# RWKV recurrence: ScalarE's instructions kept in program order, with loads, splits, statistics and one buffer rearranged

## The chip, the core and the metric

The kernel runs on one core of a Trainium2 chip. The metric is the device time of one execution in microseconds (us). The engines are named as in the profile: PE is TensorE (PEld its weight loads), DVE is VectorE, ACT is ScalarE, POOL is GpSimd, and SP is SyncE, whose queue issues the DMAs. A line number such as L1520 is a line of the kernel before the change.

## The reference

The reference is one inference step of a two-layer decoder trunk on 1,104 tokens: 8 sample sequences of 8 tokens, 16 meta tokens and a prompt of 1,024 tokens. Layer 0 is a gated DeltaNet, layer 1 is RWKV-7. The change touches the second half of layer 1 only: the recurrence over the tokens, the normalisation of its output, the output projection, and the final norm. What it computes, per head of 64 channels:

```python
def step(S, inp):
    r_t, k_t, v_t, d_t, kk_t, b_t = inp
    S = (S * d_t[:, :, None, :]
         + jnp.einsum('bhvk,bhk->bhv', S, -kk_t)[..., None] * b_t[:, :, None, :]
         + v_t[..., None] * k_t[:, :, None, :])
    return S, jnp.einsum('bhvk,bhk->bhv', S, r_t)

S, y = lax.scan(step, S0.astype(jnp.float32), (tm(r_h), tm(k_h), tm(v_h), tm(d_h), tm(kk), tm(b_h)))
...
y = (y - mean) * lax.rsqrt(var + GN_EPS) * lnx_w.reshape(H, N) + lnx_b.reshape(H, N)
y = y + jnp.sum(r_h * k_h * r_k, -1, keepdims=True) * v_h
y = y.reshape(B, T, D) * jax.nn.silu(z)
return y @ w_o, S, xn[:, -1]
```

The residual is added to the result, and a final RMSNorm gives the outputs.

## The kernel before

**Stages.** Layer 0 and the projections of layer 1 fill the first 1,890 us or so. Then comes `wave` (L1832), which is where the change lies. It works on 24 units: 3 segments of the tokens (`SEGS`, 384, 384 and 336 columns) times 8 pairs of heads. A unit has 6 chunks of 64 tokens. Step `tau` of the wave works on up to three units at once: unit n enters at step 2n and takes one chunk in each of six steps, so there are 52 steps (0 to 51), after some that only prepare.

**One step.** `step_solve` (L1457) multiplies the keys with the states S into a PSUM tile X, which ACT copies (L1478). `parts[0]` then computes half the score matrices of a coming unit on PE (`scores`, tile `G`; DVE masks them, L1386 and L1388). `step_inner` multiplies X by a triangular inverse `rTT` and ACT writes the result, UV (L1490). `step_old` scales the old states on ACT (`pre`, L1499). `step_state` (L1501) multiplies UV into new states and outputs; DVE writes the states (L1520), ACT copies the outputs y (L1528) into a ring of 8 steps. `parts[1]` and `parts[2]` hold the rest of a coming unit's preparation: the bonus term (L1371), transposed values and keys (ACT copies, L1410 and L1397).

**A unit's front and finish.** `rwkv_front` (L1330) is a generator. Up to its first `yield` (L1358) it issues the four loads of a unit (`fld2c`, `fldrv`, `AR`, `BK`), two exponentials on ACT (`fDp`, `fiD`, L1247 and L1248) and two products on DVE (L1353, L1356). It runs at the end of each even step (`front`, L1938). Its second part, one step later, makes `pr` on DVE and splits it in two on ACT and POOL (L1362, L1364). `rwkv_finish` (L1530) begins at the end of a unit's last step: twelve statistics instructions on DVE (L1540, L1541), a power of -0.5 on POOL (L103) and three DVE instructions of a Newton step (L104 to L106), then `gnm` (L1546). In the next steps ACT normalises six pieces of y (L1549), PE transposes them (`fyT`), DVE applies gain, bonus and gate (L1558, L1559), and `split` makes the two halves that the projection reads.

**Samples.** For the first 8 units, `rwkv_sample_read` loads the sample sequences' states in 8 DMAs (`sn`, L1579), and `rwkv_sample_write` (L1604) spreads UV over the sequences (`ue`, one half on POOL and one on DVE, L1609), multiplies (`drsw`, L1614), updates the states on DVE, transposes them, copies them on ACT (L1623) and stores them in 8 DMAs (L1627). The copy uses a tile of the tag `ue`, which has two buffers in all.

**Work that fills the steps.** `jobs` and `more` (L1861, L1865) are generators with a start and an end in units of `tau`; `fill(now)` advances each in proportion. They are the last gate projection (`gate_tiles`, PSUM tile `zz`, result `zst`), the output projection (`project_out`, tiles `zo` and `do`) and the final norm (`finish`). Their weights come from `stream` (L209): each block of weights is loaded into `wraw` (two buffers), ACT rounds it to `whi`, and POOL computes the rest `wlo` (three buffers each).

**What sets the order.** PE's instructions keep the order in which the program names them: the wave stands in `with tc.manual_schedule(engines={mybir.EngineType.PE})` (L1826). For all other engines, and for SP's DMAs, the compiler's scheduler picks at each point of a simulated timeline the ready instruction that was named first, and waits are inserted between engines. On the chip each engine runs its own list in order. `tc.high_priority()` lets a few instructions go ahead.

Of the kernel before, what the change touches and what calls it, by code (L numbers as in the profile page):

```python
# [7 lines left out]
F32R = mybir.dt.float32r  # L8
# [27 lines left out]
class Builder:  # L36
# [8 lines left out]
    def t(self, pool, shape, tag, bufs=1, dt=F32):  # L45
        self.uid += 1
        return pool.tile(shape, dt, name=f"{tag}_{self.uid}", tag=tag, bufs=bufs)
# [41 lines left out]
        e = nc.gpsimd if eng_lo == "pool" else nc.vector  # L89
        e.tensor_tensor(lo, x, hi.bitcast(F32), op=ALU.subtract)  # L90

    def rsqrt(self, y, x, pool, tag, bufs=2):

        v = self.nc.vector
        p0, sh = x.start_partition(), list(x.shape)
        n = 1
        for d in sh[1:]:
            n *= d
        t = self.t(pool, [p0 + sh[0], n], tag + "_t", bufs)[p0:p0 + sh[0]]
        t = t.rearrange("p (a b) -> p a b", b=sh[2]) if len(sh) == 3 else t  # L100
        half = self.cv(-0.5, p0, sh[0])
        half = half.unsqueeze(2) if len(sh) == 3 else half
        self.nc.gpsimd.tensor_tensor(y, x, half.broadcast_to(sh), op=ALU.pow)  # L103
        v.tensor_tensor(t, y, y, op=ALU.mult)  # L104
        v.scalar_tensor_tensor(t, t, -0.5, x, op0=ALU.mult, op1=ALU.mult)
        v.scalar_tensor_tensor(y, t, 1.5, y, op0=ALU.add, op1=ALU.mult)  # L106
# [82 lines left out]
    def load_w(self, src, kt=8, into=None):  # L189

        nc = self.nc
        n = src.shape[1]
        v = src.rearrange("(k p) m -> p k m", p=128)
        his, los = [], []
        for h in range(0, kt, 4):
            w = self.t(self.wp, [128, 4, 128], "wraw", 2)
            m = min(4, kt - h)
            nc.sync.dma_start(w[:, 0:m, 0:n], v[:, h:h + m, :])
            if into:
                hi, lo = into[0][h // 4], into[1][h // 4]  # L200
            else:
                hi = self.t(self.wp, [128, 4, 128], "whi", 3, F32R)
                lo = self.t(self.wp, [128, 4, 128], "wlo", 3, F32R)
            self.split(w[:, 0:m, 0:n], hi[:, 0:m, 0:n], lo[:, 0:m, 0:n], eng_lo="dve" if into else "pool")
            his.append(hi)
            los.append(lo)
        return his, los

    def stream(self, srcs):  # L209

        w = []
        for n in range(len(srcs)):
            for q in range(len(w), min(n + 3, len(srcs))):
                w.append(self.load_w(srcs[q], srcs[q].shape[0] // 128))
            yield w[n][0][0], w[n][1][0]

    def dense(self, w, m, xh, xl, seg, kt=8, tag="d", bufs=2, label=""):

# [1111 lines left out]
    def rwkv_front(self, p, s):  # L1330

        nc, t, ap, fp, col = self.nc, self.t, self.ap, self.fp, self.pcol
        P = Ctx()
        P.p, P.s, P.n = p, s, 8 * s + p
        NB = self.NB
# [4 lines left out]
        def system():  # L1340
            nc.sync.dma_start(P.TT.rearrange("p c k -> p (c k)"), self.ttd[(P.n + 1) // 5][:, 384 * (P.n - max(5 * ((P.n + 1) // 5) - 1, 0)):][:, 0:384])
        ld = self.rwkv_load(P.n, fp, "f", ("2c", "rv"))
        Dp, iD = self.rwkv_decays(ld, fp, "f")
        DC = P.DC = t(fp, [128, 14], "DC", NB + 2)
        nc.gpsimd.tensor_copy(DC[:, 0:6].unsqueeze(2), Dp[:, 1:385].rearrange("p (c k) -> p c k", k=64)[:, :, 63:64])
        if s == 0:
            nc.gpsimd.tensor_copy(DC[:, 6:14].unsqueeze(2), Dp[:, 1:65].rearrange("p (c k) -> p c k", k=8)[:, :, 7:8])
        AR = P.AR = t(fp, [128, 2, 6, 64], "AR", NB + 1)
        BK = t(fp, [128, 6, 2, 64], "BK", 2)
        nc.sync.dma_start(AR[:, 0].rearrange("p c k -> p (c k)"), self.abd[P.n][:, 0:384])  # L1350
        nc.sync.dma_start(BK[:, :, 1, :], self.abd[P.n][:, 384:768].rearrange("p (c k) -> p c k", k=64))
# [149 lines left out]
    def step_state(self, W):  # L1501
# [25 lines left out]
        if lo < hi:  # L1527
            nc.scalar.copy(y[:, lo:hi].rearrange("p c k -> p (c k)"), W.pY[:, 64 * lo:64 * hi])  # L1528

    def rwkv_finish(self, p, s, P):  # L1530

        nc, t, ap, col = self.nc, self.t, self.ap, self.pcol
        c0, n = SEGS[s]
        y = lambda q: self.ring_y(2 * P.n + q)[:, 2 - q // 2]
        zg = t(ap, [128, 384], "lz", 2)
        nc.sync.dma_start(zg, self.zd[p][:, c0:c0 + 384])
        st = t(ap, [128, 6, 6], "bnst", 2)
        mv = t(ap, [128, 6, 2], "mv", 2)
        for q in range(6):
            nc.vector.bn_stats(st[:, q, :], y(q))  # L1540
            nc.vector.bn_aggr(mv[:, q, :], st[:, q, :])  # L1541
        va, rs = t(ap, [128, 6], "va", 2), t(ap, [128, 6], "grs", 2)
        nc.vector.tensor_scalar(va, mv[:, :, 1], GN_EPS, None, op0=ALU.add)
        self.rsqrt(rs, va, ap, "gn")
        nm = t(ap, [128, 6], "gnm", 2)
        nc.vector.scalar_tensor_tensor(nm, mv[:, :, 0], -1.0, rs, op0=ALU.mult, op1=ALU.mult)  # L1546
        yield
        for q in range(6):
            self.act(y(q), y(q), AF.Identity, scale=rs[:, q:q + 1], bias=nm[:, q:q + 1])  # L1549
            if q in (3, 5):  # L1550
                yield
        yp = self.ps("f", 2, "yT")
        for q in range(6):
            for h in (0, 64):
                g = 64 - h
                self.mm(yp[h:h + 64, 64 * q:64 * q + 64], y(q)[g:g + 64], self.ident[g:g + 64, g:g + 64])
        t1 = t(self.fp, [128, 384], "k2", 1)
        nc.vector.scalar_tensor_tensor(t1[:, 0:n], yp[:, 0:n], self.lnw[:, p:p + 1], P.bv[:, 0:n], op0=ALU.mult, op1=ALU.add)  # L1558
# [45 lines left out]
    def rwkv_sample_write(self, p, P, BT, DC):  # L1604
        nc, t, ap = self.nc, self.t, self.ap
        UV = self.ring_uv(2 * P.n)[:, 2]
        ue = [t(self.fin, [128, 8, 64], "ue", 2) for h in (0, 1)]
# [11 lines left out]
        op = self.ps("d", 2, "sbT")  # L1619
        for g in range(4):  # L1620
            self.transpose(op[:, 128 * g:128 * g + 128], P.Sb[:, 2 * g:2 * g + 2, :].rearrange("p b k -> p (b k)"))
        so = t(self.fin, [128, 4, 2, 64], "ue", 2)
        nc.scalar.copy(so.rearrange("p g h k -> p (g h k)"), op)  # L1623
        st = self.o["s_rwkv"][0].rearrange("(g u) h v k -> u v g h k", u=2)
        for u in (0, 1):
# [37 lines left out]
    def finish(self, s, x2):  # L1663
        nc, t, i, o, fp = self.nc, self.t, self.i, self.o, self.fin
        for q in range(3):
            tt = 3 * s + q
            nr = 80 if tt == 8 else 128
            tag = [("d", 2), ("f", 2), ("r", 3)][q] if s == 2 else ("d", 2)
# [7 lines left out]
            r, rs = t(self.fin2, [128, 1], "fr", 2), t(self.fin2, [128, 1], "frs", 2)  # L1676
            nc.vector.tensor_tensor(r[0:nr], r2[0:nr, 0:1], r2[0:nr, 1:2], op=ALU.add)
            nc.vector.tensor_scalar(r[0:nr], r[0:nr], 1.0 / D, RMS_EPS, op0=ALU.mult, op1=ALU.add)
            self.rsqrt(rs[0:nr], r[0:nr], self.fin2, "fn")
            yp, ys = o["y_prompt"][0], o["y_sample"].rearrange("b r d -> (b r) d")  # L1680
            for h in (0, 1):
                hs = slice(512 * h, 512 * h + 512)
# [109 lines left out]
    def layer1(self, ctx, right, stay, xa, xb, x):  # L1792

        nc, tc = self.nc, self.tc
# [28 lines left out]
        self.ys = t(ap, [128, self.RING, 3, 64], "y")  # L1823
        self.TTz = [t(ap, [128, 6, 64], f"rTT{q}") for q in range(3)]
        nc.vector.memset(self.UVs, 0.0)
        with tc.manual_schedule(engines={mybir.EngineType.PE}):  # L1826
            self.wave(zin, stay, last, pool)
        last.close()
        ctx.close()
# [2 lines left out]
    def wave(self, zin, stay, last, pool):  # L1832
# [22 lines left out]
        def norms(s):  # L1855
            x = self.sums_in(s)
            yield
            yield
            yield from self.finish(s, x)
# [2 lines left out]
                (lambda: out(2, Z), 16, 30, 38), (lambda: out(3, DD), 16, 38, 46), (lambda: out(4, Z), 16, 46, 51),  # L1862
                (lambda: out(5, DD, x2), 16, 52.1, 54), (lambda: out(6, DD, x2), 8, 54.1, 55), (lambda: self.finish(2, x2), 4, 55, 56)]

        more = [(lambda: norms(0), 5, 31, 36), (lambda: norms(1), 5, 47, 51), (lambda: x2.extend(self.sums_in(2)) or iter(()), 1, 51.6, 52)]  # L1865
        runs = {}

        def fill(now):
# [15 lines left out]
                    del runs[id(jl)]  # L1884

        late = []
        def front(tau):

            if tau % 2 and (tau + 3) // 2 < 24:
                s, p = divmod((tau + 3) // 2, 8)  # L1890
                begun.append(self.rwkv_front(p, s))
                P[8 * s + p] = next(begun[-1])

        begun = []
        front(-3)
        for tau in range(-3, 55):
            m = (tau + 2) // 2
            parts = P[m].parts[3 * (tau % 2):3 * (tau % 2) + 3] if 0 <= m < 24 else [[], [], []]
# [10 lines left out]
            with self.tc.issue_after(ins) if W else ExitStack():  # L1909
# [31 lines left out]

# [28 lines left out]
```

## Time and profile before

| | us |
|---|---|
| median of 3 runs (2340.41 to 2344.61) | 2343.65 |
| the profiled execution | 2352.16 |
| its span, first to last instruction | 2350.4 |
| PE busy, of the span | 2161.4 |
| ACT busy | 1272.2 |
| DVE busy | 1603.1 |
| first and last ACT copy of X in the wave (steps 1 and 51) begin at | 1898.9 and 2304.7 |

Times inside the execution are counted from the span's start. "Busy" is the time in which an engine had an instruction in work, and the busy times of engines overlap. A row of the timeline gives the start, the duration, the engine, the line, the operation, the tile written and the tiles read, shapes, a count, and in brackets how long the engine was idle before it and what ended that. A row of the waits gives who waited for whom, the total in us, the number of times and the longest. A row of the windows gives, for one stretch of time, each engine's busy time and count of instructions, then the granted PE clock (1.00 is full), the share of DMA time used and GB/s.

### The profile page before, as it was taken

To read this page: it belongs to the slowest core of one execution; us is meant where nothing else is said; L and a number is where in the kernel's file an instruction comes from. 1 tells how busy PE (TensorE), PEld (TensorE's weight loads), DVE (VectorE), ACT (ScalarE), POOL (GpSimd) and SP (SyncE) were. 2 spreads that over 40 slices of the span, in tenths; PEclk is the share of its full clock that TensorE was granted. 3 is DMA by queue.
4 is the path that set the end of the run, shared out by engine and by line. 5 is a ranking of instruction groups with operands and counts; after the bars stand their busy time and mean duration, and the time that the engine had idled before them with its cause. 6 is when DMAs were issued, how large, how long until landed. Compare 5 with 4: busy or idle time off the path is not lost. (4 is left out here: it accounts for less than half of the span.)

```text
span 2350.4 us, 55277 instructions
## 1 busy us (share of the span) xinstructions
PE 2161.4 (92%) x20452; PEld 1966.9 (84%) x20452; DVE 1603.1 (68%) x4224; ACT 1272.2 (54%) x3642; POOL 926.3 (39%) x1267
## 2 busy tenths in 40 slices
PE   6989999999999999999999999988889988999986
PEld 5888989989888889888998989888778966788875
DVE  6868768685858677684336765878969355677754
ACT  5445555465554655566433554746545345577763
POOL 3435334343434334444231442644434333344443
PEclk9999999999999999999999999999989989999998
DMA  3324233423333333327244146654552644577754
GB/s 113 99 75 112 80 90 79 110 62 101 87 89 108 88 92 76 106 76 199 68 130 114 55 123 216 201 162 146 154 150 79 192 114 131 161 224 224 209 163 135
DMA packets 433128, 293.37 MB, mean 125 GB/s; under 512 B 148329, under 2 KB 415706, under 8 KB 432858
## 3 DMA queue, kind: packets, MB, share of 16 engines
q1 hardware_dynamic: 432858, 289.84, 43.0%
q8 instruction: 161, 2.64, 0.5%
q14 instruction: 109, 0.89, 0.1%
HBM read 198.02 MB, written 91.71 MB: 123 GB/s over the span
## 5 line engine op out<-in xcount | busy, mean ns | idle before, releaser
L90 POOL TENSOR_TENSOR wlo<-wraw,whi 128x512 fp32r<-128x512 f32 (+2 forms) x252 | 332.0, 1320 | 367.1 <-ACT whi L86 346.6
L76 PE MATMUL d<-xc,whi 128*128 128x384 f32 (+2 forms) x910 | 263.7, 346 | 7.0 <-DVE key L1168 2.2
L86 ACT CAST whi<-wraw 128x512 fp32r<-128x512 f32 (+2 forms) x252 | 151.7, 604 | 123.8 <-PE dq L76 50.5
L415 DVE SCALAR_TENSOR_TENSOR cvy<-raw,cw,cvy 128x408 f32<-128x408 f32 (+2 forms) x288 | 179.6, 637 | 17.1 <-ACT cvy L62 15.3
L76 PEld LDWEIGHTS d<-xc,whi 128*128 128x128 f32 (+1 forms) x910 | 170.9, 194 | 14.3 <-issue 4.1
L451 DVE TENSOR_TENSOR invtmp<-invA,invT 72x31 f32<-72x31 f32 (+31 forms) x403 | 167.0, 414 | 11.4 <-DMA invA<-ltd 4.6
L453 DVE TENSOR_TENSOR invT<-invT,invtmp 72x31 f32<-72x31 f32 (+31 forms) x403 | 170.1, 422 | 6.7
L76 PE MATMUL dz<-xc,whi 128*128 128x384 f32 (+1 forms) x480 | 150.1, 344 | 0.0
L76 PE MATMUL dv<-xc,whi 128*128 128x384 f32 (+1 forms) x480 | 146.7, 334 | 0.0
L76 PE MATMUL d<-xc,wlo 128*128 128x384 f32 (+2 forms) x428 | 145.5, 346 | 0.5 <-POOL wlo L90 0.5
L76 PE MATMUL d<-xa,whi 128*128 128x384 f32 (+3 forms) x450 | 142.1, 349 | 3.2 <-DVE xa L90 1.8
L815 POOL TENSOR_SCALAR Sb<-Sb,eglb 128x128 f32<-128x128 f32 x128 | 80.5, 648 | 89.8 <-DMA Sb<-in_state_gdn 39.5
L76 PE MATMUL dz<-xa,whi 128*128 128x384 f32 (+1 forms) x288 | 101.3, 352 | 0.0
L76 PE MATMUL dv<-xa,whi 128*128 128x384 f32 (+1 forms) x288 | 99.9, 347 | 0.1
L76 PEld LDWEIGHTS d<-xa,whi 128*128 128x128 f32 (+1 forms) x450 | 85.5, 194 | 7.9 <-issue 2.4
L76 PEld LDWEIGHTS dz<-xc,whi 128*128 128x128 f32 x480 | 90.2, 193 | 0.8
L76 PEld LDWEIGHTS dv<-xc,whi 128*128 128x128 f32 x480 | 88.5, 188 | 0.5 <-issue 0.4
L76 PE MATMUL d<-xl,whi 128*128 128x384 f32 (+1 forms) x256 | 84.4, 345 | 3.5 <-DVE xl L90 3.0
L76 PE MATMUL d<-xa,wlo 128*128 128x384 f32 (+3 forms) x252 | 86.8, 344 | 0.0
L76 PE MATMUL d<-xh,wlo 128*128 128x384 f32 (+1 forms) x256 | 84.7, 345 | 1.7 <-POOL wlo L90 1.7
L62 ACT ACTIVATE o<-rA,gcol 128x128 f32<-128x128 f32 x128 | 46.7, 373 | 72.7 <-DVE S L726 72.1
L62 ACT ACTIVATE attn<-attn,gcol 128x128 f32<-128x128 f32 x144 | 46.6, 391 | 72.2 <-POOL attn L526 72.1
(512 smaller groups left out, 7060.8 us busy)
## 6 DMA issues: line engine op xcount, KB each, us to landing
wraw<-in_gdn_w_in SPq DMA_DIRECT2D x96, 256.0 KB
wraw<-in_rwkv_w_rkvz SPq DMA_DIRECT2D x80, 256.0 KB
Sb<-in_state_gdn SPq DMA_DIRECT2D x64, 256.0 KB
sldcak<-cakd SPq DMA_DIRECT2D x24, 576.0 KB
cakd<-ev SPq DMA_DIRECT2D x56, 192.0 KB
wraw<-in_rwkv_w_o SPq DMA_DIRECT2D x40, 256.0 KB
E<-drow SPq DMA_DIRECT2D x24, 384.0 KB
attn<-drow SPq DMA_DIRECT2D x24, 384.0 KB
```

Of the source, the lines that this page charges most:

```text
L62: return self.nc.scalar.activation(out, in_, func, bias=bias, scale=scale, **kw)
L76: self.nc.tensor.matmul(out, lhsT, rhs, start=start, stop=stop)
L86: nc.scalar.copy(hi, x)
L90: e.tensor_tensor(lo, x, hi.bitcast(F32), op=ALU.subtract)
L415: nc.vector.scalar_tensor_tensor(y[:, 0:wd], raw[:, k:k + wd], cw[k], y[:, 0:wd], op0=ALU.mult, op1=ALU.add)
L451: nc.vector.tensor_tensor(tmp, A[:, j, j + 1:32].unsqueeze(2).broadcast_to([nb, n, m]), Tv[:, j, 0:m].unsqueeze(1).broadcast_to([nb, n, m] ...
L453: nc.vector.tensor_tensor(Tv[:, j + 1:32, 0:m], Tv[:, j + 1:32, 0:m], tmp, op=ALU.subtract)
L815: nc.gpsimd.tensor_scalar(Sb[:, u], Sb[:, u], self.eglb[:, hv, 4 * g + u:4 * g + u + 1], None, op0=ALU.mult)
```

## The change

1. ACT's instructions in the wave, like PE's, now keep the order in which the program names them.
2. `stream` names the load of a weight block two blocks ahead of its split, the splits staying two blocks ahead of their use. `wraw` keeps its two buffers.
3. `rwkv_front` yields once more: a unit's four loads are named at the end of an odd step, and its exponentials and products at the end of the even step that follows, where they were.
4. The output statistics are named in every step (`y_stats`) instead of six at a time in `rwkv_finish`; their tiles get 4 buffers instead of 2.
5. The power on POOL and the Newton step on DVE are parted (`later=True`): in `rwkv_finish` the Newton step and `gnm` come at the start of the next step, in `finish` (segments 0 and 1) one turn later. `norms` takes 8 turns instead of 5 in the same stretch of steps. At the end of an odd step, the turn of `rwkv_finish` with `fyT` is named ahead of the statistics.
6. The copy of the sample states gets a tile of its own (`ssn`, one buffer).

```diff
-    def rsqrt(self, y, x, pool, tag, bufs=2):
+    def rsqrt(self, y, x, pool, tag, bufs=2, later=False):
...
         self.nc.gpsimd.tensor_tensor(y, x, half.broadcast_to(sh), op=ALU.pow)
+        if later:
+            return lambda: self.newton(y, x, t)
+        self.newton(y, x, t)
+
+    def newton(self, y, x, t):
+
+        v = self.nc.vector
         v.tensor_tensor(t, y, y, op=ALU.mult)
         v.scalar_tensor_tensor(t, t, -0.5, x, op0=ALU.mult, op1=ALU.mult)
         v.scalar_tensor_tensor(y, t, 1.5, y, op0=ALU.add, op1=ALU.mult)
...
     def stream(self, srcs):
 
-        w = []
+        raw, w = [], []
         for n in range(len(srcs)):
-            for q in range(len(w), min(n + 3, len(srcs))):
-                w.append(self.load_w(srcs[q], srcs[q].shape[0] // 128))
-            yield w[n][0][0], w[n][1][0]
+            while len(raw) < min(n + 5, len(srcs)):
+                q = len(raw)
+                if q > 1 and len(w) < q - 1:
+                    x, m, c = raw[len(w)]
+                    hi, lo = (self.t(self.wp, [128, 4, 128], a, 3, F32R) for a in ("whi", "wlo"))
+                    self.split(x[:, 0:m, 0:c], hi[:, 0:m, 0:c], lo[:, 0:m, 0:c])
+                    w.append((hi, lo))
+                raw.append(self.load_w(srcs[q], srcs[q].shape[0] // 128, later=True))
...
+            yield w[n]
...
         ld = self.rwkv_load(P.n, fp, "f", ("2c", "rv"))
+        AR = P.AR = t(fp, [128, 2, 6, 64], "AR", NB + 1)
+        BK = t(fp, [128, 6, 2, 64], "BK", 2)
+        nc.sync.dma_start(AR[:, 0].rearrange("p c k -> p (c k)"), self.abd[P.n][:, 0:384])
+        nc.sync.dma_start(BK[:, :, 1, :], self.abd[P.n][:, 384:768].rearrange("p (c k) -> p c k", k=64))
+        yield P
+
         Dp, iD = self.rwkv_decays(ld, fp, "f")
...
+    def y_stats(self, items, tau):
+
+        nc, t = self.nc, self.t
+        y = self.ring_y(tau)
+        for P, ci in items:
+            if ci == 0:
+                P.st, P.mv = t(self.ap, [128, 6, 6], "bnst", 4), t(self.ap, [128, 6, 2], "mv", 4)
+            nc.vector.bn_stats(P.st[:, ci, :], y[:, 2 - ci // 2])
+        for P, ci in items:
+            nc.vector.bn_aggr(P.mv[:, ci, :], P.st[:, ci, :])
...
-        self.rsqrt(rs, va, ap, "gn")
+        newton = self.rsqrt(rs, va, ap, "gn", later=True)
+        yield
+        newton()
         nm = t(ap, [128, 6], "gnm", 2)
         nc.vector.scalar_tensor_tensor(nm, mv[:, :, 0], -1.0, rs, op0=ALU.mult, op1=ALU.mult)
-        yield
...
-        so = t(self.fin, [128, 4, 2, 64], "ue", 2)
+        so = t(self.fin, [128, 4, 2, 64], "ssn", 1)
...
-            self.rsqrt(rs[0:nr], r[0:nr], self.fin2, "fn")
+            newton = self.rsqrt(rs[0:nr], r[0:nr], self.fin2, "fn", later=True)
+            if s < 2:
+                yield
+            newton()
...
-        with tc.manual_schedule(engines={mybir.EngineType.PE}):
+        with tc.manual_schedule(engines={mybir.EngineType.PE, mybir.EngineType.Activation}):
...
-        more = [(lambda: norms(0), 5, 31, 36), (lambda: norms(1), 5, 47, 51), (lambda: x2.extend(self.sums_in(2)) or iter(()), 1, 51.6, 52)]
+        more = [(lambda: norms(0), 8, 31, 36), (lambda: norms(1), 8, 47, 51), (lambda: x2.extend(self.sums_in(2)) or iter(()), 1, 51.6, 52)]
...
+                if tau % 2 and 0 <= (tau - 7) // 2 < 24:
+                    next(P[(tau - 7) // 2].done)
+                if W:
+                    self.y_stats(items, tau)
                 for Q, ci in items:
                     if ci == 5:
                         Q.done = self.rwkv_finish(Q.p, Q.s, Q)
                         next(Q.done)
-                if tau % 2 and 0 <= (tau - 7) // 2 < 24:
-                    next(P[(tau - 7) // 2].done)
-                front(tau + 1)
+                if tau % 2:
+                    load((tau + 5) // 2)
+                else:
+                    front()
```

More of the change, by code (lines that the diff above doesn't have):

```diff
@@ L90, in split @@
         e.tensor_tensor(lo, x, hi.bitcast(F32), op=ALU.subtract)
-    def rsqrt(self, y, x, pool, tag, bufs=2):
-        v = self.nc.vector
+    def rsqrt(self, y, x, pool, tag, bufs=2, later=False):
         p0, sh = x.start_partition(), list(x.shape)
@@ L187, in open_weights, with load_w @@
         self.wp = ctx.enter_context(self.tc.tile_pool(name="weights", bufs=1))
-    def load_w(self, src, kt=8, into=None):
+    def load_w(self, src, kt=8, into=None, later=False):
         nc = self.nc
@@ L198, in load_w @@
             nc.sync.dma_start(w[:, 0:m, 0:n], v[:, h:h + m, :])
+            if later:
+                return w, m, n
             if into:
@@ L209, in stream @@
     def stream(self, srcs):
-        w = []
+        raw, w = [], []
         for n in range(len(srcs)):
-            for q in range(len(w), min(n + 3, len(srcs))):
-                w.append(self.load_w(srcs[q], srcs[q].shape[0] // 128))
-            yield w[n][0][0], w[n][1][0]
+            while len(raw) < min(n + 5, len(srcs)):
[6 more added lines that the diff above has]
+                raw.append(self.load_w(srcs[q], srcs[q].shape[0] // 128, later=True))
+            while len(w) < min(n + 3, len(srcs)):
+                x, m, c = raw[len(w)]
+                hi, lo = (self.t(self.wp, [128, 4, 128], a, 3, F32R) for a in ("whi", "wlo"))
+                self.split(x[:, 0:m, 0:c], hi[:, 0:m, 0:c], lo[:, 0:m, 0:c])
+                w.append((hi, lo))
+            yield w[n]
     def dense(self, w, m, xh, xl, seg, kt=8, tag="d", bufs=2, label=""):
@@ L1347, in rwkv_front @@
             nc.gpsimd.tensor_copy(DC[:, 6:14].unsqueeze(2), Dp[:, 1:65].rearrange("p (c k) -> p c k", k=8)[:, :, 7:8])
[L1348 to L1351, printed above, removed]
         c6 = lambda x: x.rearrange("p (c k) -> p c k", k=64)
@@ L1536, in rwkv_finish @@
         nc.sync.dma_start(zg, self.zd[p][:, c0:c0 + 384])
[L1537 to L1541, printed above, removed]
+        mv = P.mv
         va, rs = t(ap, [128, 6], "va", 2), t(ap, [128, 6], "grs", 2)
         nc.vector.tensor_scalar(va, mv[:, :, 1], GN_EPS, None, op0=ALU.add)
-        self.rsqrt(rs, va, ap, "gn")
+        newton = self.rsqrt(rs, va, ap, "gn", later=True)
+        yield
+        newton()
         nm = t(ap, [128, 6], "gnm", 2)
         nc.vector.scalar_tensor_tensor(nm, mv[:, :, 0], -1.0, rs, op0=ALU.mult, op1=ALU.mult)
-        yield
         for q in range(6):
@@ L1886, in wave, with load, front @@
         late = []
[L1887 to L1895, printed above, removed]
+        loaded, begun = [], []
+        def load(n):
+            if n < 24:
+                loaded.append(self.rwkv_front(n % 8, n // 8))
+                P[n] = next(loaded[-1])
+        def front():
+            if loaded:
+                begun.append(loaded.pop(0))
+                next(begun[-1])
+        load(0)
+        front()
         for tau in range(-3, 55):
@@ L1935, in wave @@
                         next(Q.done)
-                if tau % 2 and 0 <= (tau - 7) // 2 < 24:
-                    next(P[(tau - 7) // 2].done)
-                front(tau + 1)
+                if tau % 2:
+                    load((tau + 5) // 2)
+                else:
+                    front()
         fill(99)
```

## The prediction

> **What bounds the kernel now.** I read the page first, for the engines' shares, then the windows of the stage that the change touches, then the waits of PE in it, and last the timeline around the longest of these waits.
>
> ```profile
> PE 2161.4 (92%) x20452; PEld 1966.9 (84%) x20452; DVE 1603.1 (68%) x4224; ACT 1272.2 (54%) x3642; POOL 926.3 (39%) x1267
> ```
> ```profile
> 1895.00:2045.00 150.00, 130.50 (x1834) 105.64 (x1835) 94.15 (x305) 78.73 (x227) 54.28 (x62) 0.94 0.49 137
> 2045.00:2300.00 255.00, 240.13 (x3775) 204.51 (x3773) 175.36 (x602) 178.40 (x536) 112.01 (x118) 1.00 0.69 202
> ```
>
> PE carries the time: 92% of the span. The wave divides into two stretches. In the later one (second row: length, then PE, PEld, DVE, ACT and POOL busy, PE's granted clock) PE works 240.1 of 255 us at full clock; 14.9 us are all that any reordering can win there. In the earlier one, while sample sequences are handled, PE works 130.5 of 150 us, at a clock of 0.94: 19.5 us are open in little more than half the length. So I look for the gain there, and ask who makes PE wait.
>
> ```profile
> PE drsw L76 <- DVE xss L1602: 8.1, 5, 3.6
> PE zz L76 <- DVE zst L984: 3.7, 2, 2.8
> PE drsw L76 <- DVE ue L1609: 2.0, 2, 1.6
> PE fG L76 <- ACT BT L1397: 2.0, 4, 0.6
> PE drsw L76 <- DVE bnst L1540: 1.9, 2, 1.4
> DVE ue L1609 <- DMA out_s_rwkv<-ue: 14.4, 7, 3.7
> ```
>
> These waits (total, times, longest) are of the wave. Three of PE's five end in `drsw`, the product that updates a sample state: 8.1 + 2.0 + 1.9 = 12.0 us in 9 waits. The releaser named is mostly DVE's copy `xss`, a small one. The last row says why a small copy is late: DVE itself stood 14.4 us for the store of the previous unit's sample states. The timeline around the longest case:
>
> ```profile
> 1951.98 5.40 SPq L1627 DMA_DIRECT2D out_s_rwkv<-ue  x7
> ...
> 1955.45 0.27 DVE L1518 TENSOR_SCALAR rS<-rS,DC 128x64 f32<-128x64 f32 x1
> 1958.79 0.69 DVE L1609 TENSOR_TENSOR ue<-UV,bmask 128x512 f32<-128x512 f32 x1 [3.07 <-DMA out_s_rwkv<-ue]
> ...
> 1960.21 0.34 DVE L1602 COPY xss<-drsr 128x64 f32<-128x64 f32 x2
> ```
> ```profile
> 1956.67 0.34 PE L76 MATMUL drsr<-ident,rkst 64*64 64x64 f32 x8
> 1960.57 1.97 PE L76 MATMUL drsw<-ue,BT 128*64 128x512 f32 x4 [3.55 <-DVE xss L1602]
> ```
>
> `ue` and the copy that is being stored share two buffers. DVE's next `ue` waits 3.07 us for the store; statistics and `xss` queue behind it, and PE stands 3.55 us between `drsr`, which `xss` reads, and `drsw`.
>
> **The change part by part.** All sums are made against the profiled execution, 2352.16 us (span 2350.4), and then carried to the median of 2343.65, which is 8.5 lower.
>
> *The states' own buffer* takes the store out of `ue`'s way. What is left of the bubble is the round trip from `drsr` over `xss` to `drsw`. The first unit, which has no store before it, shows it:
>
> ```profile
> 1905.18 1.08 PE L76 MATMUL drsw<-ue,BT 128*64 128x512 f32 x4 [0.41 <-DVE xss L1602]
> 1920.52 1.08 PE L76 MATMUL drsw<-ue,BT 128*64 128x512 f32 x4 [1.81 <-DVE xss L1602]
> 2020.28 1.76 PE L76 MATMUL drsw<-ue,BT 128*64 128x512 f32 x2 [1.62 <-DVE ue L1609]
> ```
>
> Nine times 0.41 is 3.7, so **8.3 us** of the 12.0 go. The store now holds up only the next copy into `ssn`, one unit later. A unit takes 150 / 8 = 18.8 us here and the eight stores of one unit are issued in about 6 us, so that wait should be zero. If the store were late, ACT, now in fixed order, would stand for it with everything behind it (`y`, `BT`, X); the price is bounded by DVE's row above, 0 to 14.4 us, and I take 0.
>
> *PE's clock.* The bubbles cost twice, as the windows after four of them show (clock in the third number from the end):
>
> ```profile
> 1920.00:1925.00 5.00, 4.48 (x56) 3.54 (x56) 2.59 (x11) 0.27 (x1) 0.00 (x0) 0.66 0.41 98
> 1931.00:1936.00 5.00, 4.95 (x59) 4.21 (x59) 1.26 (x8) 1.07 (x3) 0.00 (x0) 0.66 0.26 72
> 1960.50:1966.50 6.00, 5.93 (x68) 3.88 (x68) 3.30 (x12) 0.27 (x1) 0.96 (x1) 0.55 0.91 260
> 2020.00:2025.00 5.00, 4.72 (x62) 2.96 (x64) 3.33 (x15) 0.09 (x1) 1.32 (x1) 0.66 1.04 316
> ```
>
> Three windows lose 0.34 of 5 us, one 0.45 of 6: 5.1 + 2.7 = 7.8 us of clock. Without bubbles of 1.6 to 3.6 us it should not fall. Not all of that time is bound by PE's rate, so I take two thirds, **5.2 us**; the bounds are 0 and 7.8. [...]
>
> *ACT in program order.* The exponentials `fDp` and `fiD` now come last in the even step, behind the gate's `zst`, the other copies and `BT`. Before, the scheduler put them first:
>
> ```profile
> 1926.67 0.51 ACT L62 ACTIVATE fiD<-fld2c 128x384 f32<-128x384 f32 x1
> 1927.21 0.45 ACT L62 ACTIVATE zst<-zz 128x336 f32<-128x336 f32 x1
> ```
> ```profile
> 1927.64 1.40 DVE L1356 TENSOR_TENSOR BK<-fld2c,fiD 128x384 f32<-128x384 f32 x1
> 1928.96 1.61 DVE L1362 SCALAR_TENSOR_TENSOR pr<-fldrv,pcol,fld2c 128x384 f32<-128x384 f32 x1
> 1930.50 0.49 DVE L984 SCALAR_TENSOR_TENSOR zst<-zst,zz 128x336 f32<-128x336 f32 x1
> ```
>
> DVE's products of the front (3.0 us for these two) stood ahead of `zst`, for which PE waited 2.8 us. With the products later, `zst` goes first: **2.5 us** of the 3.7 in two waits. In every pair of steps the exponentials also made `BT` late, for which a PSUM buffer of `fG` waits:
>
> ```profile
> 2121.66 0.51 ACT L62 ACTIVATE fiD<-fld2c 128x384 f32<-128x384 f32 x1
> 2122.41 0.48 ACT L1397 COPY BT<-fBT 128x384 f32<-128x384 f32 x1
> 2122.78 0.34 ACT L1478 COPY X<-rX 128x192 f32<-128x192 f32 x1
> ```
> ```profile
> 2122.62 1.25 PE L76 MATMUL fG<-AR,BK 64*128 64x128 f32 x12
> 2130.39 0.94 PE L76 MATMUL fG<-AR,BK 64*128 64x128 f32 x12
> ```
>
> With `BT` ahead of them, 1.5 of the 2.0 us of outright waits go, and of the 0.31 us by which `fG` is stretched in each of some 18 later pairs I count a third: **2 us** (bounds 0 and 5.6), since X, which follows all of it, must still be there when `fG` ends. The sum of ACT's work ahead of X is the same in both orders, so X should be no later.
>
> *Loads and splits.* The named place moves, the DMAs remain the same. The order on the chip already has it: a unit's load stands in the odd step, its exponential in the even one after.
>
> ```profile
> 2125.38 0.38 SPq L1235 DMA_DIRECT2D fld2c<-cakd  x1
> ...
> 2135.40 0.52 ACT L62 ACTIVATE fDp<-fld2c 128x384 f32<-128x384 f32 x1
> ```
>
> Ten us lie between. I cost this at nothing; the cover is that distance, and without it PE would wait a DMA's latency per pair. `wraw` has two buffers as before, so no weight can arrive earlier than its buffer is free. That holds at the start of the wave too, where PE stands longest:
>
> ```profile
> 1885.84 1.65 PE L76 MATMUL fG<-AR,BK 64*128 64x128 f32 x10 [5.35 <-ACT BT L1397]
> 1887.00:1894.00 7.00, 7.00 (x66) 6.12 (x65) 2.21 (x7) 1.88 (x4) 0.00 (x0) 0.50 0.40 108
> ```
>
> `BT` stands there behind a split whose weights are late, and in program order it still does. With its seven us at half clock (second row) this is 5.35 + 3.5 = 8.9 us; the fixed order may shorten it by all of this, or lengthen it by as much if the first splits now wait for the last copies of the stage before. I take 0 and keep both ends.
>
> *Statistics and Newton steps.* As many instructions as before. The statistics run in DVE's gaps (175 of 255 us busy). The Newton step no longer holds DVE while POOL computes the power; in exchange ACT's normalisation waits for it in the next step. Price 0, if DVE runs it straight after the masks `G`; the opposite case is a rival below. The turns of `norms` shift some transposes, no more; 0.
>
> **Sum:** 8.3 + 5.2 + 2.5 + 1.5 + 2 = 19.5 us. I give back 4.5 for what is late next. In the sample steps it is SP: it issues 16 sample DMAs per unit at the median below, 9.7 us, and some ten others, an estimated 5, against a unit that would shrink from 18.8 us to about 16.8 (17.5 us over eight units). That is near enough to full for some loads to come late.
>
> ```profile
> L1627 SPq DMA_DIRECT2D out_s_rwkv<-ue x64: 597/606/2121, 1912.1 to 2054.6; - x64
> ```
>
> So 15 us are won: the profiled execution would take 2337, the median **2328.7, say 2329 us**.
>
> **The rivals.** A measurement of this kernel tells about 0.2%, 4.7 us, from no change.
>
> *The clock does not come back* (0.10). If the half-rate stretches have another cause than these bubbles, the 5.2 us fall away: 2334. For it: the clock at the wave's start recovers late. Against: each low window follows a bubble directly.
>
> *The start is repaired too* (0.12). If the loads named earlier get ahead of the sample loads on SP, up to 8.9 us more go: about 2320, at the ends of the other terms 2314. Against it: `wraw` still has two buffers.
>
> *The next wait takes its place* (0.15). SP or another DVE instruction holds `xss`, and only the removal of outright `BT` and `zst` waits stays: 1.5 + 2.5 us, about 2340, which counts as no change. For it: DVE's list is full of waits, and 14.4 us of waiting gave only 12.0 of PE's.
>
> *ACT blocks on the Newton step* (0.20), the rival on the other side. The rows of an even step:
>
> ```profile
> 2116.36 0.17 DVE L1546 SCALAR_TENSOR_TENSOR gnm<-mv,grs 128x6 f32<-128x6 f32 x1
> 2119.29 0.55 DVE L1371 TENSOR_TENSOR rbv<-fldrv,fbonus 128x384 f32<-128x384 f32 x1 [1.58 <-PE fbonus L76]
> ```
> ```profile
> 2118.99 1.42 ACT L62 ACTIVATE y<-y,gnm,grs 128x64 f32<-128x64 f32 x4
> ```
>
> Now `gnm` is ready 2.5 us before ACT reads it. If the scheduler puts the Newton step behind `rbv`, its four instructions of 0.17 end at about 2120.6 and ACT starts 1.6 us late; the split of weights, `y`, `BT` and X queue behind it. PE's work between X and its use covers some 0.7 (X is written by 2123.1, `fG` runs to 2123.9), so each of 24 finishing units costs 0.9 us: 22 - 15 = 7 us slower than before, 2351. It decides from the point where `gnm` is over 0.7 us late. Against it: the Newton step is named ahead of `rbv`, and its input is ready a step earlier, while DVE idles 1.58 us just there.
>
> **How the numbers follow.** The forecast with its own range of 2321 to 2337 has 0.43, the rivals 0.10, 0.12, 0.15 and 0.20. Faster by over 0.2%: 0.43 + 0.10 + 0.12 = 0.65; within: 0.15; slower: 0.20. The range of 8 in 10 runs from 2314, the lower end of the second rival, to 2352, which leaves out about half of the slower case and little below.
>
> **What would show it.** Right: no wait of `ue` for the store; `drsw` bubbles of about 0.4; the windows of the sample stretch at a clock near 1; units of 16 to 17 us there; `fG` of 0.94 in odd steps, and `BT` ahead of `fDp` in ACT's list. Wrong: ACT idle ahead of `y<-y` for `gnm`; ACT idle ahead of the sample copy for `out_s_rwkv`; PE waiting for X; or SP's queue without gaps with `rTT`, `sn` or `wraw` late. If the later stretch, 255 us now, moves by more than 5 us either way, I have mistaken what the fixed order does.

## The result, and the profile after

| | before | after |
|---|---|---|
| median of 6 runs each, side by side, us | 2340.44 (2335.51 to 2344.61) | 2325.68 (2323.31 to 2327.45) |
| ratio after/before, 95% interval | | 0.9936 [0.9919, 0.9953] |
| profiled execution, us | 2352.16 | 2324.47 |
| its span, us | 2350.4 | 2322.5 |

The kernel became faster, by 14.8 us of the medians. 2329 was forecast, as a gain of about 15.

The two spans differ by 27.9 us, nearly twice as much, and the first question is why. The first `zz` product of the wave stands at 1868.97 us before and at 1854.03 after: 15 us lie ahead of the wave, where the engines' lists of instructions are the same in both kernels but for their last few entries. So these 15 us are a difference between two executions (the runs of the old kernel beside the experiments reached from 2327.65 to 2355.92 us, and the profiled one is near their upper end), and the change has to be read from the wave alone. I cut the wave, from that first `zz` on, at ACT's copies of X in steps 1, 16, 32, 46 and 51:

| kernel | to step 1 | 1 to 16 (samples) | 16 to 32 | 32 to 46 | 46 to 51 | 51 to end | wave |
|---|---|---|---|---|---|---|---|
| before | 30.0 | 142.7 | 118.0 | 106.5 | 38.6 | 45.7 | 481.5 |
| after | 27.6 | 132.0 | 116.9 | 103.1 | 39.3 | 49.5 | 468.4 |
| difference | -2.4 | -10.7 | -1.1 | -3.4 | +0.7 | +3.8 | -13.1 |

These 13.1 us agree with the medians. Most of them lie in the sample stretch; 4.5 lie in the thirty steps behind it, and 4.5 are lost again in the last steps and the end.

The page's shares after, then the windows of the sample stretch and of the later one (length, busy PE, PEld, DVE, ACT, POOL, then the clock):

```profile
PE 2144.8 (92%) x20452; PEld 1955.3 (84%) x20452; DVE 1594.6 (69%) x4224; ACT 1271.5 (55%) x3642; POOL 924.5 (40%) x1267
```
```profile
1880.00:2015.00 135.00, 120.68 (x1801) 99.66 (x1801) 90.43 (x296) 75.84 (x217) 51.73 (x60) 0.96 0.54 148
2015.00:2270.00 255.00, 240.44 (x3802) 206.02 (x3797) 167.22 (x608) 180.21 (x542) 109.71 (x117) 0.99 0.69 205
```

The shares say nothing: 92% before, 92% after. The stretch says more: PE works 120.7 of 135 us there, so 14.3 are open instead of 19.5, and the clock rose only from 0.94 to 0.96. The waits of the wave show who holds PE now:

```profile
DVE ue L1638 <- ACT UV L62: 6.4, 4, 3.7
PE rX L80 <- DMA rTT<-ttd: 6.3, 6, 3.1
PE do L76 <- ACT yh L86: 6.0, 2, 4.4
PE drsw L76 <- DVE xss L1631: 5.5, 7, 1.1
PE zz L76 <- DVE zst L1003: 4.3, 2, 3.4
```

Before, two of these rows were smaller:

```profile
PE rX L80 <- DMA rTT<-ttd: 2.3, 3, 1.3
PE do L76 <- ACT yh L86: 2.0, 2, 1.5
```

`ue` no longer waits for a store at all, but for its operand `UV`. The bubbles ahead of `drsw` fell from 12.0 to 5.5 us, the longest from 3.6 to 1.1. First among the new ones is a load: PE waits 6.3 us for `rTT`, where it was 2.3. The longest of these waits, on PE and on SP:

```profile
1916.69 1.08 PE L76 MATMUL drsw<-ue,BT 128*64 128x512 f32 x4 [1.08 <-DVE xss L1631]
...
1923.35 0.36 PE L80 MATMUL rX<-X,rTT 64*64 64x64 f32 x1 [3.12 <-DMA rTT<-ttd]
```
```profile
1907.81 6.47 SPq L1656 DMA_DIRECT2D out_s_rwkv<-ssn  x8
1914.38 0.54 SPq L204 DMA_DIRECT2D wraw<-in_rwkv_w_rkvz  x1
1914.96 5.63 SPq L1608 DMA_DIRECT2D sn<-in_state_rwkv  x7
1920.70 0.54 SPq L1360 DMA_DIRECT2D rTT<-ttd  x1
1921.33 0.38 SPq L204 DMA_DIRECT2D wraw<-in_rwkv_w_rkvz  x1
```
```profile
1923.00:1929.00 6.00, 5.65 (x38) 5.11 (x39) 2.06 (x3) 4.08 (x11) 1.04 (x1) 0.50 0.81 237
```

SP issues eight stores and seven loads of sample states, 12.1 us of issuing with one load of weights between them, and the small load of the inverse, `rTT`, is behind them. It is issued at 1920.70; PE wanted it 0.5 us earlier and gets it 3.12 us late. Its tile, one of three buffers, had come free by 1911.6, with the last product of the unit three before it; the 9 us from there are SP's queue. The bubble ahead of `drsw` is 1.08 where it was 1.81. The third fence is the price that follows: six us at half clock. The bubble moved from DVE's queue to SP's.

In the steps behind the samples, ACT's order is the one that the prediction named (`BT`, then the exponentials, then X), and `fG` runs at 0.94 in it and in the step after:

```profile
2092.85 0.48 ACT L1418 COPY BT<-fBT 128x384 f32<-128x384 f32 x1
2093.23 0.53 ACT L62 ACTIVATE fDp<-fld2c 128x384 f32<-128x384 f32 x1
2093.65 0.51 ACT L62 ACTIVATE fiD<-fld2c 128x384 f32<-128x384 f32 x1
2094.07 0.31 ACT L1499 COPY X<-rX 128x192 f32<-128x192 f32 x1
```
```profile
2093.75 0.94 PE L76 MATMUL fG<-AR,BK 64*128 64x128 f32 x12
2101.20 0.94 PE L76 MATMUL fG<-AR,BK 64*128 64x128 f32 x12
```

At the end of the wave the mechanism of the slower rival is there, twice (ACT waits 2.25 and 4.75 us for `gnm`). The longer case:

```profile
2279.99 1.43 ACT L62 ACTIVATE y<-y,gnm,grs 128x64 f32<-128x64 f32 x4 [4.75 <-DVE gnm L1576]
2281.33 0.45 ACT L86 CAST yh<-lz 128x336 fp32r<-128x336 f32 x1
...
2281.84 0.65 PE L76 MATMUL do<-yh,whi 128*128 128x336 f32 x1 [4.44 <-ACT yh L86]
```

ACT stands 4.75 us for `gnm`; `yh`, whose input `lz` was written by 2278.0, stands behind it in the fixed order, and PE waits 4.44 us for `yh`. Before, the scheduler took `yh` first:

```profile
2309.85 0.47 ACT L86 CAST yh<-lz 128x336 fp32r<-128x336 f32 x1 [2.22 <-DVE lz L1559]
2310.53 2.10 ACT L62 ACTIVATE y<-y,gnm,grs 128x64 f32<-128x64 f32 x6 [0.21 <-DVE gnm L1546]
```

### The profile page after: what moved, and what is told of

It is laid out like the page before. It is cut to its first block, busy times and chain, and to the rows that moved or that the text cites. A ratio compares the mean times of both kernels' runs of the same rounds, so it can differ in the third digit from the quotient of the medians.

```text
span 2322.5 us, 55260 instructions
## 1 busy us (share of the span) xinstructions
PE 2144.8 (92%) x20452; PEld 1955.3 (84%) x20452; DVE 1594.6 (69%) x4224; ACT 1271.5 (55%) x3642; POOL 924.5 (40%) x1267
## 5 line engine op out<-in xcount | busy, mean ns | idle before, releaser
L76 PEld LDWEIGHTS d<-xc,whi 128*128 128x128 f32 (+1 forms) x910 | 170.7, 194 | 14.4 <-issue 3.8
L76 PEld LDWEIGHTS dz<-xc,whi 128*128 128x128 f32 x480 | 88.7, 190 | 0.8
L76 PEld LDWEIGHTS dv<-xc,whi 128*128 128x128 f32 x480 | 88.5, 188 | 0.5 <-issue 0.4
L76 PE MATMUL d<-xh,whi 128*128 128x384 f32 (+1 forms) x256 | 85.3, 346 | 0.4 <-ACT xh L86 0.2
```

What stands on the lines that cost most here:

```text
L76: self.nc.tensor.matmul(out, lhsT, rhs, start=start, stop=stop)
```

## The experiments

Theory A, that of the prediction: the gain is two edits. The states' own buffer frees `drsw` and gives most; ACT's order gives the rest behind the samples; all else costs and gives nothing. Against it stands, first, that the own buffer gives little by itself, because another instruction of DVE holds `xss` or SP comes next, so that ACT's order carries the change; and second, that the parted Newton step or the earlier loads take part, for better or worse. Each ratio is against the old kernel run beside it on the same chip.

**e1, the own buffer alone**, in the old kernel:

```diff
-        so = t(self.fin, [128, 4, 2, 64], "ue", 2)
+        so = t(self.fin, [128, 4, 2, 64], "ssn", 1)
```

> The kernel before with one edit: the copy of the sample states gets its own tile (ssn). Theory A (the gain is the store taken out of the way of ue, with the clock that the bubbles cost): most of the prediction's 8.3 + 5.2 us less what is late next, so 9 us faster than before (7 to 13), ue no longer waits for the store, drsw bubbles at 0.4 us. Theory B (the gain is ScalarE's order): at most 3 us faster, because the bubbles in front of drsw only move to the next late instruction of VectorE.

Measured: 2331.81 us, ratio 0.9955 [0.9932, 0.9977]: by the ratio 10.5 us are won. In the waits:

```profile
PE drsw L76 <- DVE xss L1602: 3.0, 5, 1.2
PE rX L80 <- DMA rTT<-ttd: 2.8, 4, 1.1
...
PE drsw L76 <- DVE bnst L1540: 0.9, 2, 0.5
```

The bubbles of `drsw` sum to 3.9 (0.56 each, where 0.4 was expected), and the sample stretch takes 133.5 us instead of 142.7. `rTT` is hardly later than before. The rival by which the buffer gives little falls.

**e2, the changed kernel without the own buffer** (the edit of e1 undone in it):

> The changed kernel with only the own buffer undone (the copy goes back to the tag ue). Theory A: 9 us of the 15 are lost again, so 4 to 7 us faster than the kernel before; VectorE's ue waits for the store some 14 us again. Theory B: still about 13 us faster.

Measured: 2342.27 us, ratio 0.9995 [0.9979, 1.0012]: nothing is won. The waits are the old ones, somewhat longer:

```profile
DVE ue L1638 <- DMA out_s_rwkv<-ue: 18.9, 7, 4.0
PE drsw L76 <- DVE xss L1631: 7.6, 5, 2.9
PE drsw L76 <- DVE bnst L1558: 4.7, 2, 3.2
```

Without the buffer the other edits gain 3.2 us between steps 32 and 46, and lose as much at the end. In sum they give nothing, where A expected 4 to 7 us of them: a miss.

**e3, the changed kernel with ACT's order free**, and **e4, ACT's order fixed in the old kernel**. e4 is this edit in the old kernel, e3 its reverse in the changed one:

```diff
-        with tc.manual_schedule(engines={mybir.EngineType.PE}):
+        with tc.manual_schedule(engines={mybir.EngineType.PE, mybir.EngineType.Activation}):
```

> The changed kernel with ScalarE's order left to the scheduler again. Theory A: loses the terms of the order, 6 us (2.5 + 1.5 + 2), so about 9 us faster than before; fG is stretched to 1.25 us again in the odd steps after the samples. Theory B: about as fast as before (0 to 3 us faster).

> The kernel before with one edit: ScalarE's instructions in program order, everything else as before. Theory A: about 5 us faster (2 to 7): zst and BT come earlier, the store still holds ue. Theory B: 12 us faster or more. A third possibility: slower than before, if the loads, named right before their splits and exponentials, now stop ScalarE; then the moved loads are what the fixed order needs.

Measured: e3 2335.16 us, 0.9972 [0.9952, 0.9992]; e4 2335.71 us, 0.9978 [0.9959, 0.9997]. The order is worth some 5 us by itself and 8 in the changed kernel (-15.0 by ratio with it, -6.5 without). Two of e3's waits:

```profile
PE rX L80 <- DMA rTT<-ttd: 9.0, 7, 2.3
PE fG L76 <- ACT BT L1418: 5.8, 3, 4.4
```

The stretched `fG` is back in some of e3's steps, at 1.27 to 1.33 us, as expected. Of its 5.8 us for `BT`, though, 4.4 stand at the start of the wave and 1.4 in the sample stretch, none behind it. By stages, e4 wins 6.8 us in the sample stretch and 1.8 between steps 16 and 46, and loses 4.4 from step 46 on. e3 keeps the old end (82.7 us from step 46, against 84.3 before and 88.8 after), but needs 10.9 more than the changed kernel between 16 and 46: PE is busy 5.8 us longer there (217.3 against 211.5), 3.4 of them because its clock spends 6.8 us at half rate, and it waits 4.2 us longer for `rTT`. The gain before the end goes with the fixed order in every profile: between 16 and 46 PE is busy 215.8 to 217.3 us in the three kernels whose ACT order is free (before, e1, e3), and 211.1 to 212.9 in the nine with it fixed. The loss at the end is less clear: 82.7, 84.3 and 87.0 us with the order free, 85.9 to 88.9 with it fixed.

**e5, the inverse named early.** The load of `rTT` moves from its own turn in step order to the place where the front's other loads are named, one and a half steps earlier; its tile gets five buffers instead of three:

```diff
-        def system():
-            nc.sync.dma_start(P.TT.rearrange("p c k -> p (c k)"), ...)
+        nc.sync.dma_start(P.TT.rearrange("p c k -> p (c k)"), ...)
...
-        P.parts = [[lambda: scores(0)], [bonus], [lambda: keys(0)], [lambda: scores(3)], [system, values], [lambda: keys(3)]]
+        P.parts = [[lambda: scores(0)], [bonus], [lambda: keys(0)], [lambda: scores(3)], [values], [lambda: keys(3)]]
...
-        self.TTz = [t(ap, [128, 6, 64], f"rTT{q}") for q in range(3)]
+        self.TTz = [t(ap, [128, 6, 64], f"rTT{q}") for q in range(5)]
```

> The changed kernel, with the triangular inverse rTT loaded with the unit's other loads (end of an odd step, one and a half steps earlier) into five buffers instead of three. If the waits of PE for rTT (6.3 us in the changed kernel's profile, 2.3 before) are what the faster sample steps ran into, they go, with the half-rate stretch after the longest: 5 to 8 us faster than the changed kernel, so 19 to 23 us faster than before. If SyncE's queue is simply full, another load is late instead and the time stays within 3 us of the changed kernel's.

Measured: 2315.46 us, 0.9893 [0.9860, 0.9925], by the ratio 25 us below the old kernel, more than the 19 to 23 expected. It is 9 below the changed kernel, for which e6 and e8, both at 2324 to 2325 on the same chip, have to stand. No wait for `rTT` is left:

```profile
PE do L76 <- ACT yh L86: 6.0, 2, 4.4
PE zz L76 <- DVE zst L1003: 5.8, 2, 4.9
PE drsw L76 <- DVE xss L1630: 4.4, 6, 1.1
```
```profile
1880.00:2003.00 123.00, 115.48 (x1791) 95.85 (x1789) 89.44 (x294) 75.27 (x217) 52.05 (x60) 1.00 0.57 157
```

The sample stretch shrinks by 11.5 us, from 132.0 to 120.5, at a clock of 1.00. PE is idle 6.8 us less there (7.5 instead of 14.3), of which 4.8 are the waits for `rTT` that lay in this stretch, and busy 4.7 us less (113.0 instead of 117.7), where the clock had lost 5.1. The loss that I had put down loosely as "some loads come late" was this one load. It still stands behind a row of sample loads:

```profile
1914.62 4.92 SPq L1607 DMA_DIRECT2D sn<-in_state_rwkv  x7
1919.63 0.54 SPq L1359 DMA_DIRECT2D rTT<-ttd  x1
```

But this is the inverse of a unit whose first products with it come at 1953.25 or later, some 34 us on. In the changed kernel the inverses that were issued during the sample stretch had 5.4 us at best up to the first such product of their step, and in the case above PE already stood. Three buffers cannot give much more: a unit keeps its tile for six steps and a new one enters every second step, so the buffer comes free only one step ahead of its next use. The place and the two more buffers therefore win together; neither was run by itself, nor was the load put ahead of SP's row with three buffers.

**e6, the finished halves ahead of the Newton step**, meant to take back the end: in even steps the turn that names `yh` comes before the one with the Newton step and `gnm`.

```diff
+                if tau % 2 == 0 and 0 <= (tau - 8) // 2 < 24:
+                    next(P[(tau - 8) // 2].done, None)
...
-                if tau % 2 == 0 and 0 <= (tau - 8) // 2 < 24:
-                    next(P[(tau - 8) // 2].done, None)
```

> The changed kernel with the last turn of a finishing unit (yh, yl) named ahead of the next unit's Newton step and normalisation in an even step. If the longer end (4.5 us more from step 46 to the end in all three kernels with ScalarE in program order) comes from ScalarE standing for gnm with yh queued behind it, PE's wait of 4.4 us for yh goes: 4 us faster than the changed kernel (2 to 6). If the end is longer for another reason, no difference.

Measured: 2324.81 us, 0.9930 [0.9904, 0.9955], the changed kernel's time: a miss. The wait went as meant, and others came:

```profile
2280.18 0.42 PE L76 MATMUL do<-yh,whi 128*128 128x336 f32 x1 [1.11 <-ACT yh L86]
...
2281.73 0.42 PE L76 MATMUL do<-yl,whi 128*128 128x336 f32 x1 [1.13 <-POOL yl L90]
...
2294.32 0.42 PE L76 MATMUL do<-yh,whi 128*128 128x336 f32 x1 [2.10 <-ACT whi L86]
```

The 4.44 us became 1.11; POOL's `yl` then costs 1.13 and a split of weights, `whi`, another 2.10. From step 46 to the end it takes 88.9 us, as after (88.8). **e7, e5 and e6 together:**

> Both edits together: the sum of the two, 9 to 14 us faster than the changed kernel, 24 to 28 us faster than before, if the waits are independent.

Measured: 2315.32 us, 0.9891 [0.9862, 0.9921], the time of e5. The end gave nothing here either that can be told from scatter.

**e8, the Newton step at once**, as before the change, in the changed kernel:

```diff
-        newton = self.rsqrt(rs, va, ap, "gn", later=True)
-        yield
-        newton()
+        self.rsqrt(rs, va, ap, "gn")
...
+        yield
```

> The changed kernel with the Newton step of rwkv_finish back at the end of the unit's last step (that part of the change undone, in rwkv_finish alone). By the prediction the parted Newton step costs and gains nothing in the steady steps: within 3 us of the changed kernel. If it is what keeps VectorE from standing for GpSimd's power in the sample steps, 4 us or more slower; if it makes ScalarE wait, faster.

Measured: 2324.40 us, 0.9932 [0.9906, 0.9958]. Parting the Newton step neither gains nor loses anything that can be told from scatter.

**e9, the own buffer and ACT's order alone**, in the old kernel (the edits of e1 and e4), and **e10, those two with e5's early inverse**:

> The kernel before with two edits only: the own buffer and ScalarE's program order; loads, splits, statistics and Newton steps stay where they were. If these two carry the change and their gains add (10.5 us and 5.1 us alone), 15 us faster than before, as the changed kernel is. If the moved loads and the spread statistics are what the order needs to pay, 8 to 11 us faster, with ScalarE standing for weights or exponentials.

> The same two edits, and rTT loaded with the unit's other loads into five buffers. In this kernel these loads are named at the end of an even step, one step later than in the changed kernel, but still a step and more ahead of use. If rTT's place was all that was wrong, 25 us faster than before, as the changed kernel with the same edit; if the other moved loads matter, 18 to 21 us.

Measured: e9 2324.22 us, 0.9921 [0.9896, 0.9945]; e10 2316.90 us, 0.9884 [0.9856, 0.9912]. e9 has the time of the whole change: earlier loads and splits, spread statistics, parted Newton steps and the turns of `norms` together give no gain, and as a gain the second rival falls. As a loss it stays open. With these edits the time is longer in three pairs: by 4.0 us in e3 against e1 and 3.8 in e2 against e4 (means of twelve runs each on one chip, give or take 5 and 4 us), and by 3.5 in the changed kernel against e9 (by the ratios). Each is within scatter, but they point the same way. e10 is 7 us below e9 and not to be told from e5, so the two edits, with the inverse named early into five buffers, are the version that beats both kernels.

| kernel | to step 1 | 1 to 16 | 16 to 46 | 46 to end | wave | `drsw` waits | `rTT` waits |
|---|---|---|---|---|---|---|---|
| before | 30.0 | 142.7 | 224.5 | 84.3 | 481.5 | 12.0 | 2.3 |
| after | 27.6 | 132.0 | 220.0 | 88.8 | 468.4 | 5.5 | 6.3 |
| e1 own buffer | 29.3 | 133.5 | 227.1 | 87.0 | 476.9 | 3.9 | 2.8 |
| e4 order | 27.3 | 135.9 | 222.7 | 88.7 | 474.6 | 13.2 | 3.1 |
| e9 both | 27.5 | 128.5 | 220.0 | 88.5 | 464.5 | 4.4 | 4.9 |
| e5 early inverse | 30.4 | 120.5 | 218.8 | 88.4 | 458.2 | 4.9 | 0 |

Each row is one profiled execution, so differences of up to some 4 us between rows are not told from scatter; the medians carry the verdicts.

## Why the prediction was right, point by point

**The own buffer, 8.3 us forecast.** Right in mechanism, a little too large: the bubbles fell by 6.5 us in the changed kernel, by 8.1 in e1. I took 0.41 for what is left of each. Four of the seven left are 1.05 to 1.08, because on DVE the statistics now stand between `drsr` and `xss`:

```profile
1956.50 0.34 PE L76 MATMUL drsr<-ident,rkst 64*64 64x64 f32 x8
1956.86 0.48 DVE L1558 BATCH_NORM_STATS2 bnst<-y 128x6 f32<-128x64 f32 x3 [1.31 <-ACT y L1549]
1957.26 0.30 DVE L1560 BATCH_NORM_AGGREGATE mv<-bnst 128x2 f32<-128x6 f32 x3
...
1957.54 0.35 DVE L1631 COPY xss<-drsr 128x64 f32<-128x64 f32 x2
```

So the statistics, costed at nothing, hold PE for some 0.6 us in four units. e9, without their spreading, has 4.4 us of `drsw` waits against 5.5, with two of its seven at 1.2; in the medians it can't be seen. The store as a new obstacle for the copy into `ssn` did not appear, and 0 was right there.

**PE's clock, 5.2 us forecast.** Right in direction, too large. In the sample stretch the clock record shows 17.1 us at half rate before, 10.2 after and none in e5: 8.5 us of rate lost, then 5.1, then none. The step failed in size at the new bubble ahead of `rTT`, which took a stretch of 6.8 us at half rate, 3.4 us of rate, for itself. That bubbles of 1.6 us and more cost clock, as I had read from four windows, the runs bear out. Counted over the start of the wave and the sample stretch of all twelve profiles, 31 of 33 bubbles of 1.6 us and more were followed by a stretch at half rate that began 1.9 to 4.9 us after the bubble did; of 54 bubbles between 0.7 and 1.6 us, four at most were. In the profiles before and after alone these are seven of eight (the eighth, the 1.97 us ahead of 2001.14 before, was followed by none until the bubble of 1.62 us, 19 us later) and none of ten. Two stretches at half rate had no bubble of 0.7 us in the five us ahead of them: one in e10 and, in the changed kernel, the one that begins at 1963.69, with idle times of 0.60 and 0.47 us just ahead of it.

**`zz` for `zst`, 2.5 us forecast.** The long wait of the sample stretch (2.8) went, as argued; 0.93 of the 3.7 stays. But the sum of this wait is 4.3 after, because one came that I had not named, at the start of the wave:

```profile
1860.49 0.62 ACT L86 CAST whi<-wraw 128x512 fp32r<-128x512 f32 x1 [2.91 <-DMA wraw<-in_rwkv_w_rkvz]
1861.01 0.44 ACT L62 ACTIVATE zst<-zz 128x336 f32<-128x336 f32 x1
...
1862.05 0.65 PE L76 MATMUL zz<-xa,whi 128*128 128x336 f32 x1 [3.37 <-DVE zst L1003]
```

The fixed order puts a split that waits for its weights ahead of `zst`, whose input `zz` was written by 1858.7. In return the 5.35 us of waiting for `BT` are gone. Together the start moved from 30.0 to 27.6; I had taken 0 with 8.9 either way, and neither end came.

**`BT` and `fG`, 1.5 + 2 us forecast.** Right in mechanism, too small in size. The 2.0 us of waits for `BT` are gone (the 0.2 that is left stands at the start of the wave), but 1.4 of them lay in the sample stretch. From step 16 to 46 the kernel is 4.5 us shorter, and most of that is `fG` itself, which takes 0.94 in nearly every step where it often took 1.25 or more. Here are the windows of this stretch for the instructions on `fG` alone (length, busy PE, PEld and DVE, clock), before and after:

```profile
2041.61:2266.10 224.49, 31.93 (x360) 25.32 (x360) 29.87 (x60) 1.00 0.71 209
2013.67:2233.70 220.03, 28.53 (x360) 22.79 (x360) 30.42 (x60) 1.00 0.72 213
```

These are 3.4 us in 30 steps, where I had counted a third of the stretching, 2 us, for 36: most of the stretching was time lost. The bound of 5 us that I set for the later stretch held.

**The 4.5 given back.** Half right in place and too small. SP's queue was named, and the load that was late is `rTT`: 4.0 us more waiting. What I had put at nothing is the end: 4.5 us more from step 46 on in these two profiles. There the slower rival's mechanism occurs, ACT standing for `gnm` with `yh` behind it. In the 24 finishing units on which I put 0.9 us each it stays covered; its two cases are late in the wave (2.25 and 4.75 us), where, as I read it, no further unit's work lies beside it. e4 has the same end (88.7 us) with the Newton step in its old place, and e8 shows no difference, so it is the fixed order and not the parted Newton step; how much of the 4.5 is the order stays uncertain, since e1, with ACT's order free, has 87.0. That removing this wait would win the 4.4 us is not so: e6 removed 3.3 of it and PE waited for `yl` and `whi` instead. What bounds the end otherwise stays open.

**Loads, splits, statistics, Newton: 0 forecast.** No gain came of them, as e8 and e9 show. That they cost nothing is not shown: the three pairs named under e10 leave room for up to some 4 us.

So the mechanisms were right, and that the sum met the time was in part luck. The gains came to 6.5 (`drsw`) + 3.4 (clock) + 2.8 (`zst`) + 2.0 (`BT`) + 3.4 (`fG`) = 18.1 us, where 19.5 stood. The losses were 4.0 (`rTT`) + 4.5 (end) = 8.5, where 4.5 stood. The start, taken as 0, won 2.4. That makes 12.0 of the wave's 13.1. In the sample stretch the terms can be set against PE's idle and busy time, before and after:

```profile
1898.93:2041.61 142.68, 123.28 (x1772) 99.39 (x1772) 87.67 (x290) 74.19 (x214) 50.53 (x57) 0.94 0.49 136
1881.66:2013.67 132.01, 117.69 (x1764) 97.10 (x1761) 88.89 (x290) 74.31 (x214) 51.49 (x60) 0.96 0.53 147
```

PE's idle time fell by 5.1 us: 6.5, 2.8 and 1.4 less for `drsw`, `zst` and `BT`, 4.8 more for `rTT`, and 1.2 more in a wait of `fG` for `k`, which was not there before. Its busy time fell by 5.6, of which the clock explains 3.4; the rest is not assigned.

## What to carry to other kernels

When a compute tile shares its buffers with a tile that a DMA stores from, the engine's next write waits for the store (here 14.4 us of waiting): look in the waits for an engine that waits for a DMA *out*, and trace which small copy queues behind it. When such a wait goes, the stretch gets shorter and another queue comes next, here SP's (6.3 us of waiting for `rTT`, where it was 2.3). Before changing the order of engines, look at what that queue issues last, and at how long before its use the buffer of a small load comes free; an earlier place for the load can need more buffers (here the two together were worth 7 to 9 us, beside 15 for the whole change). An order fixed by hand paid here in the repeating middle (from step 16 to 46 PE is busy 211.5 us in the changed kernel, where it was 215.8), and has to be looked at separately where the pattern ends.

## What the hardware showed that I had not expected

PE's clock fell after an idle time of 1.62 us in the sample stretch (ahead of 2020.28 before), and after one of 1.41 us at the end of the wave (ahead of 2308.74 before). In the profiles before and after, each stretch at half rate in the waves was 3.41, 6.83 or 10.24 us, but for the last one, which runs past the end of the span; so a bubble of 1.81 us, with 3.41 us at half rate behind it, cost up to 1.7 us more. Bubbles between 0.7 and 1.6 us were mostly free of that at the start of the wave and in the sample stretch (four of 54 at most were followed by half rate).

Two executions differed by 15 us in a part in which their instructions are the same but for the last few. A difference of two spans is therefore no measure of an edit; stages cut at the same instruction are, and the medians above them.
